# The MLP's first product by one level of Strassen's scheme, chunk after chunk

## The chip, the cores and the metric

The kernel runs on one core of a Trainium2 chip. Its time is the device time of one execution in microseconds: 1842.22 us, the median of three runs (1840.79 to 1843.36). TensorE (PE) multiplies matrices; VectorE (DVE), ScalarE (ACT) and GpSimd (POOL) do elementwise work; the queue of SyncE (SP) issues the transfers between DRAM and the on-chip memory SBUF. Each of the five has one stream of instructions and takes it in order. Sums of matrix products arise in PSUM, of which a bank holds 512 float32 values on each of 128 partitions.

## The reference

One layer of an encoder over 1536 tokens (512 of a prompt, 1024 of a sample) and 1024 channels, in float32:

```python
h = h + concat(o_attn, o_pool) @ w_out
m = rmsnorm(h, norm_mlp_g)
h = h + square(relu(m @ w_up)) @ w_down          # w_up 1024x4096, w_down 4096x1024
gate = sigmoid(rmsnorm(h, norm_ple_g) @ w_ple_gate)
h = h + gate * (p_i @ w_ple_proj)
```

Ahead of it stand a norm, an input projection, attention and a pooling mixer; behind it a final norm.

## The kernel before

Every matrix product is made as three passes of float32r matmuls: both operands are split into a high part (a cast) and a low part (the value less the cast), and high*high, high*low and low*high are summed (`three`). From the output projection on, activations lie transposed, channels on partitions: `hT[c][a]` is the residual stream of chunk c (512 tokens; chunk 0 the prompt, 1 and 2 the sample), channels 256a to 256a+255, as a tile of 128x1024. SBUF is one pool of 49 equal slots; a load into a slot waits for the slot's last reader, and loads stand in SP's queue in the order written.

`heads_out` adds the attention's rows of the output projection (`po`, matmuls of 128x256, each sum added to `h` by DVE). `mean_square(c)` squares a chunk's residual (`squares`: ACT squares, POOL sums, L581 to L591), splits the sum into `sh` (ACT L615, POOL L616), sums over partitions on TensorE (`w<-sh,ones_sb`) and takes it out by DVE (L621). The inverse root of it is not applied to the MLP's input: since the MLP is the square of a relu, the residual is multiplied by the mean square instead (`raise_h`, L630) and later by its inverse (`invert`, L637; `lower_h`, L644). `prep(c)` makes the two parts of the MLP's input (ACT L605, POOL or DVE L598); the norm's gain is multiplied into the weights (L740).

The MLP takes 32 hidden blocks f of 128 channels, and for each the three chunks in turn. `up(f, c)` is 8 x 3 matmuls of 128x512 into `pu`; ACT takes the relu (L757) and the square (L758, the high part of r), POOL squares again (L759), DVE makes the low part (L761). `down(f, c)` runs one step later: 4 x 2 x 3 matmuls of 128x512 into `pd`, and four DVE adds into the residual (L937). So a block's weights (one load of 512 KB each for up and down; split by ACT L743 and POOL L744) serve three chunks, and each is loaded once. The order of all this is written by hand in one list of pairs (f, c), with chores (generators that issue one step at a time) between.

Behind the MLP, `gate` makes the gated embedding: products `pj` and `pg` from `hg` (L1018, L1019), `wg` (L985, L986), `pp` and `wpj`; `stat_g` is the norm in front of it.

## Time and profile before

| what | value |
|---|---|
| median of runs | 1842.22 us (1840.79 to 1843.36) |
| profiled execution: span of its instructions | 1839.5 us |
| TensorE busy | 1806.2 us, 98% |
| DVE, ACT, POOL busy | 1098.3, 684.8, 652.8 us |
| MLP on TensorE, first `pu` to first `pj` | 575.05 to 1649.28 us |
| moved by DMA | 112.28 MB |

The profile page and the answers of the trace are of one execution, whose span is 1839.5 us; the runs' times are of the whole program and stand some 2.7 us above it. In a row of groups stand line, engine, operation, output and inputs, partitions x elements and the count; then busy time in us and mean ns of one (pipelined matmuls overlap, so their mean is longer than their spacing), then the idle time of the engine ahead of them and what ended it. In a timeline row stand the start and the length in us of a run of equal instructions, and in brackets the idle time ahead. "PEclk" or the clock column is the granted clock of TensorE as a share of the full one.

### The profile page before, as it was taken

The page shows a single profiled execution, that of the slowest core. Times are in us where ns is not written, and L with a number is a line of the kernel's source. Part 1 is how long each engine was busy: PE and PEld are TensorE (multiplying, and loading weights), DVE is VectorE, ACT ScalarE, POOL GpSimd, SP SyncE. Part 2 cuts the span into 40 slices and gives each one's busy share as a digit, 9 for nine tenths or more (in the row PEclk, how much of TensorE's full clock was granted, in tenths as well). Part 3 has the DMA queues.
Part 4 walks back from the last instruction along what each step waited for, and adds up shares of the span by engine and source line. Part 5 has one row for each costly group of instructions (what it writes and reads, how often), then busy time and mean ns, then how long its engine had stood idle before and what let it go on. Part 6 is the DMA issues. An engine that isn't in the chain of part 4 may idle for free.

```text
span 1839.5 us, 22941 instructions
## 1 busy us (share of the span) xinstructions
PE 1806.2 (98%) x8812; PEld 1492.1 (81%) x8812; DVE 1098.3 (60%) x1440; ACT 684.8 (37%) x1380; POOL 652.8 (35%) x611
## 2 busy tenths in 40 slices
...
DMA packets 34701, 112.28 MB, mean 61 GB/s; under 512 B 4768, under 2 KB 7200, under 8 KB 34592
## 3 DMA queue, kind: packets, MB, share of 16 engines
...
q14 instruction: 40, 0.33, 0.1%
...
## 4 chain that ended last, share of the span: by engine, by line
PE 88%; DVE 5%; issue 2%; ACT 2%; POOL 1%; DMA 0%; POOLq 0%; DVEq 0%; ACTq 0%
PE pd L49 28%; PE pu L49 27%; PE pg L49 7%; PE z L49 7%; PE o L49 3%; PE tp L53 3%; PE pp L49 3%; PE S L49 3%; PE po L49 3%; PE pj L49 2%; DVE m L598 1%; DVE wg L986 1%; DVE pt L473 1%; DVE nm L441 1%; PE py L49 0%
## 5 line engine op out<-in xcount | busy, mean ns | idle before, releaser
L937 DVE TENSOR_TENSOR h<-pd,h 128x1024 f32<-128x1024 f32 x372 | 445.9, 1219 | 497.0 <-PE pd L49 496.1
L49 PE MATMUL pd<-r,wd 128*128 128x512 f32 x2304 | 550.9, 394 | 3.2 <-DVE r L761 3.2
L49 PE MATMUL pu<-m,wu 128*128 128x512 f32 x2304 | 548.4, 393 | 0.0
L49 PEld LDWEIGHTS pd<-r,wd 128*128 128x128 f32 x2304 | 433.4, 188 | 104.9 <-DVE r L761 4.1
L49 PEld LDWEIGHTS pu<-m,wu 128*128 128x128 f32 x2304 | 432.8, 188 | 100.4
L759 POOL TENSOR_TENSOR ra<-ra 128x512 f32<-128x512 f32 x96 | 101.0, 1052 | 712.7 <-ACT r L758 702.8
L757 ACT ACTIVATE ra<-pu 128x512 f32<-128x512 f32 x96 | 57.4, 598 | 774.5 <-PE pu L49 774.5
L49 PE MATMUL z<-w,x 128*128 128x512 f32 (+1 forms) x864 | 175.9, 360 | 1.4 <-ACT w L159 1.4
L49 PEld LDWEIGHTS z<-w,x 128*128 128x128 f32 x864 | 143.7, 190 | 27.5 <-ACT w L159 2.8
L461 POOL TENSOR_SCALAR pr<-pr,rr 128x512 f32<-128x512 f32 x160 | 111.2, 705 | 128.0 <-DVE rr L456 62.8
L49 PE MATMUL pg<-hg,wg 128*128 128x512 f32 (+1 forms) x768 | 141.2, 338 | 1.8 <-POOL hg L1019 0.9
L49 PEld LDWEIGHTS pg<-hg,wg 128*128 128x128 f32 x768 | 118.4, 188 | 19.6 <-DVE wg L986 1.6
L473 DVE TENSOR_TENSOR pt<-tp,pt 128x512 fp32r<-128x512 f32 x160 | 104.0, 683 | 31.9 <-ACT pt L472 31.5
L472 ACT CAST pt<-tp 128x512 fp32r<-128x512 f32 x160 | 88.0, 591 | 86.2 <-PE tp L53 84.6
L441 DVE TENSOR_REDUCE nm<-S 128x1 f32<-128x1024 f32 (+1 forms) x96 | 100.0, 1042 | 23.6 <-PE S L49 23.0
L449 ACT ACTIVATE pr<-S,nm 128x512 f32<-128x512 f32 x160 | 109.5, 695 | 5.1 <-DVE nm L441 4.3
L744 POOL TENSOR_TENSOR wu<-wur,wu 128x1024 fp32r<-128x1024 f32 x32 | 78.2, 2443 | 80.4 <-ACT wu L743 75.9
L49 PE MATMUL o<-pt,vs 128*128 128x512 f32 x320 | 95.4, 407 | 2.6 <-DVE pt L473 2.2
L49 PE MATMUL S<-ks,qb 128*128 128x512 f32 x320 | 91.2, 398 | 1.8 <-DVE h L696 0.8
L53 PE MATMUL tp<-id_sb,pr 128*128 128x128 f32 x640 | 86.4, 273 | 3.7 <-DVE qs L343 3.3
L53 PEld LDWEIGHTS tp<-id_sb,pr 128*128 128x128 f32 x640 | 75.1, 140 | 18.1 <-issue 4.3
L761 DVE TENSOR_TENSOR r<-ra,r 128x512 fp32r<-128x512 f32 x96 | 68.7, 716 | 23.4 <-POOL ra L759 23.4
...
## 6 DMA issues: line engine op xcount, KB each, us to landing
wur<-in_w_up_dram SPq DMA_DIRECT2D x32, 512.0 KB, 3.3
wdr<-in_w_down_dram SPq DMA_DIRECT2D x32, 512.0 KB, 3.3
xn<-in_xn_dram SPq DMA_DIRECT2D x12, 512.0 KB, 6.5
qs_d<-qs SPq DMA_DIRECT2D x12, 512.0 KB, 3.0
yT_d<-y SPq DMA_DIRECT2D x12, 512.0 KB, 2.9
qb<-qs_d SPq DMA_DIRECT2D x12, 512.0 KB, 3.9
yb<-yT_d SPq DMA_DIRECT2D x12, 512.0 KB, 5.4
h<-in_xr_dram SPq DMA_DIRECT2D x12, 512.0 KB, 6.1
```

What stands on the lines that cost most here:

```text
L49: last_pe[0] = nc.tensor.matmul(*a, **k).ins
L53: last_pe[0] = nc.tensor.transpose(*a, **k).ins
L441: ve.tensor_reduce(nm, S[:, :nch * CH], axis=AX.X, op=ALU.max, negate=True)
L449: sc.activation(self.pr[j // 2, c][:, j % 2], S[:, c * CH:(c + 1) * CH], AF.Exp, bias=nm, accum_out=self.sums[:, j, c:c + 1])
L461: gp.tensor_scalar(p, p, rr, 1.0, op0=ALU.mult, op1=ALU.mult)
L472: sc.copy(self.pt[kt][:, 0], tp)
L473: ve.tensor_tensor(self.pt[kt][:, 1], tp, as32(self.pt[kt][:, 0]), op=ALU.subtract)
L744: gp.tensor_tensor(WM[f, i][1], raw, as32(WM[f, i][0]), op=ALU.subtract)
L757: sc.activation(a, pu, AF.Relu)
L759: gp.tensor_tensor(a, a, a, op=ALU.mult)
L761: low.append(lambda: ve.tensor_tensor(r[:, 1], a, as32(r[:, 0]), op=ALU.subtract))
L937: ve.tensor_tensor(hT[c][a], pd.rearrange("p (a b) -> p a b", a=2), hT[c][a], op=ALU.add)
```

## The change

The product of a pair of hidden blocks with a chunk's input is taken as a 2x2 block product: the contraction in halves of 512 channels, the hidden channels in halves of 128 (the two blocks), the tokens in halves of 256. Strassen's scheme in Winograd's form makes it of seven products of the quarters where eight are usual, with sums of the operands ahead and of the results behind. Numbers 1 to 7 name the products: each is 12 matmuls of 128x256.

- `operands(c)` makes the seven right operands of a chunk: ACT scales the normed gain into the residual copy `m` (eight steps of 128x512, L611), DVE forms the differences `t` (ten, L617), ACT casts (14, L622), POOL and DVE make the lows (seven each, L626). The gain has left the weights.
- `Pair.feed` makes the seven left operands of a pair: s1 to s4 on DVE (L785 to L796), seven casts on ACT (L778), seven lows on POOL (L779). `split_down` splits two blocks of the second product's weights (ACT L808; POOL and DVE L809).
- `Pair.run` writes the products to `px`, `py`, `pz`, `pq` (two products each add into `px`, `pz`, `pq`), ACT and DVE combine them in SBUF (`t`, u2, u4, c1, c2) and take relu, square and the low parts of r (L845 to L878).
- `Pair.down` sums the two blocks' rows of the second product in PSUM: again 48 matmuls of 128x512 per pair and chunk, with four adds (L829) where there were eight.
- Chunks run in turn: 16 pairs of chunk 0, then of 1, then of 2. All weights are loaded and split three times, 192 loads of 512 KB where there were 64. The residual of a finished chunk goes to DRAM (`hl_d`), those of the others come from there (`h_d`); the mean square goes there as soon as it is made (`w_d`, L654).
- In the last pair of chunk 0 and 1 the operands of the next chunk are made, between that pair's own steps.
- The first gate follows the last pair's `down` at once; the splits of `wpj`, `wg`, `pp` and `hg` stand between its four parts and behind them.

Three places of the order. POOL at the start of the MLP, before, from the split of block 1's weights on (`sqm` and `sh` belong to chunk 2's mean square, whose sum `w` stood on TensorE inside the third `up`; the first `up` followed the last `po` there):

```order
L744 TENSOR_TENSOR wu_1_6443<-wur_6262,wu_1_6442 128x1024
L744 TENSOR_TENSOR wd_1_6447<-wdr_6264,wd_1_6446 128x1024
L759 TENSOR_TENSOR ra_6490<-ra_6490 128x512
L589 TENSOR_TENSOR sqm_6485<-sqm_6485,sqm_6500 128x1024
L589 TENSOR_TENSOR sqm_6485<-sqm_6485,sqm_6508 128x1024
L589 TENSOR_TENSOR sqm_6485<-sqm_6485,sqm_6517 128x1024
L591 TENSOR_TENSOR sqm_6485<-sqm_6485 128x512
L759 TENSOR_TENSOR ra_6531<-ra_6531 128x512
L616 TENSOR_TENSOR sh_6573<-sqm_6485,sh_6573 128x512
```

and now, behind six lows of operands(0) (`mo_i1` is the low part of the operand of product i, `w_0_i` an operand from the weights of pair 0):

```order
L779 TENSOR_TENSOR w_0_1_6426<-wur_00_6057,w_0_1_6426 128x512
L626 TENSOR_TENSOR mo_41_6431<-t_6421,mo_40_6430 128x512
L779 TENSOR_TENSOR w_0_6_6437<-ws_00_6424,w_0_6_6437 128x512
L779 TENSOR_TENSOR w_0_2_6444<-wur_00_6057,w_0_2_6444 128x512
L589 TENSOR_TENSOR sqm_6440<-sqm_6440,sqm_6442 128x1024
L589 TENSOR_TENSOR sqm_6440<-sqm_6440,sqm_6447 128x1024
L779 TENSOR_TENSOR w_0_5_6453<-ws_00_6424,w_0_5_6453 128x512
L589 TENSOR_TENSOR sqm_6440<-sqm_6440,sqm_6450 128x1024
L591 TENSOR_TENSOR sqm_6440<-sqm_6440 128x512
L648 TENSOR_TENSOR sh_6463<-sqm_6440,sh_6463 128x512
L779 TENSOR_TENSOR w_0_7_6520<-ws_01_6425,w_0_7_6520 128x512
```

On TensorE the two matmuls `w` of chunk 2 now stand between the last `po` and the first `px`, so that POOL's `sh` is ahead of every product.

SP at the same place, before (`w_d` is stored from chunk 0's `sqm`):

```order
L56 DMA wur_6262<-in_w_up_dram 128x1024
L56 DMA wdr_6264<-in_w_down_dram 128x1024
L56 DMA wur_6741<-in_w_up_dram 128x1024
L56 DMA wdr_6743<-in_w_down_dram 128x1024
L639 DMA w_d_259<-sqm_4561 128x512
L639 DMA w_d_260<-sqm_5856 128x512
L56 DMA wur_6895<-in_w_up_dram 128x1024
L56 DMA wdr_6897<-in_w_down_dram 128x1024
L639 DMA w_d_261<-sqm_6485 128x512
```

and now (`h_d_3_273` is the last of chunk 2's residual; `h_6488` to `h_6494` are chunk 0's residual, `w_6496` its mean square, `wdr_ij` the second product's weights of pair i):

```order
L702 DMA h_d_3_273<-h_5459 128x1024
L56 DMA wur_10_6457<-in_w_up_dram 128x1024
L56 DMA wur_11_6458<-in_w_up_dram 128x1024
L56 DMA h_6488<-h_d_0_262 128x1024
L654 DMA w_d_261<-sqm_6440 128x512
L56 DMA h_6490<-h_d_1_263 128x1024
L56 DMA h_6492<-h_d_2_264 128x1024
L56 DMA h_6494<-h_d_3_265 128x1024
L56 DMA w_6496<-w_d_259 128x512
L56 DMA wdr_00_6498<-in_w_down_dram 128x1024
L56 DMA wdr_01_6499<-in_w_down_dram 128x1024
L56 DMA wdr_10_6570<-in_w_down_dram 128x1024
```

The store of chunk 2's mean square, which DVE's L653 releases, now stands ahead of the loads that the first pair needs.

DVE in the last pair of chunk 0, whose rows before had no like (a middle stretch of the same engine then: an add out of PSUM, two of each `down` ahead of the low of r):

```order
L621 TENSOR_SCALAR sqm_6485<-w_6594 128x512
L937 TENSOR_TENSOR h_6100<-pd_6606,h_6100 128x1024
L937 TENSOR_TENSOR h_6102<-pd_6614,h_6102 128x1024
L761 TENSOR_TENSOR r_6602<-ra_6601,r_6602 128x512
L937 TENSOR_TENSOR h_6104<-pd_6623,h_6104 128x1024
L937 TENSOR_TENSOR h_6106<-pd_6631,h_6106 128x1024
```

and now, from s4 of that pair to u4 (`t_9683`, `t_9686` and `mo_` belong to chunk 1's operands, `pd_140`, `pd_141` to the `down` of the pair before):

```order
L796 TENSOR_TENSOR ws_151_9510<-wur_150_9370,ws_150_9509 128x512
L626 TENSOR_TENSOR mo_11_9645<-m_1_9391,mo_10_9644 128x512
L829 TENSOR_TENSOR h_6488<-pd_140_9650,h_6488 128x1024
L850 TENSOR_TENSOR u_15_9608<-py_15_9664,u_15_9608 128x256
L617 TENSOR_TENSOR t_9683<-m_0_9390 128x512
L617 TENSOR_TENSOR t_9683<-m_1_9391 128x512
L617 TENSOR_TENSOR t_9686<-m_2_9392,t_9683 128x512
L617 TENSOR_TENSOR t_9686<-m_3_9393,t_9683 128x512
L626 TENSOR_TENSOR mo_61_9690<-t_9686,mo_60_9689 128x512
L809 TENSOR_TENSOR wd_1511_9633<-wdr_151_9492,wd_1510_9632 128x512
L626 TENSOR_TENSOR mo_21_9714<-m_3_9393,mo_20_9713 128x512
L829 TENSOR_TENSOR h_6490<-pd_141_9719,h_6490 128x1024
```

The rows of operands stand between the adds, u2 and u4; each `mo_` row waits for a cast of ACT, which in its queue stands behind the eight scales.

The diff, cut to its core:

```diff
+    def operands(c):
+        m = mraw.pop(c)
+        A, B = slice(0, HF), slice(HF, CH)
...
+        def quarter(half, tok):
+            return [m[2 * half + b][:, :, tok] for b in range(2)]
+        def scale(a, h):
+            sc.activation(m[a][:, h], m[a][:, h], AF.Copy, scale=gmlp_sb[:, 2 * a + h:2 * a + h + 1])
+        def minus(nm, x, y, b):
...
+            ve.tensor_tensor(T[nm][b], x()[b], y()[b], op=ALU.subtract)
+        def high(i, x, b):
...
+            sc.copy(MO[c][i][0][:, 2 * b:2 * b + 2], x()[b])
+        def low_(i, x, b):
+            hi, lo = (t[:, 2 * b:2 * b + 2] for t in MO[c][i])
+            (gp, ve)[b].tensor_tensor(lo, x()[b], as32(hi), op=ALU.subtract)
+        steps[0] = [lambda a=a, h=h: scale(a, h) for a in (0, 1, 2, 3) for h in range(2)]
+        b11, b12, b21, b22 = (lambda: quarter(0, A)), (lambda: quarter(0, B)), (lambda: quarter(1, A)), (lambda: quarter(1, B))
+        t = [lambda i=i: T[i] for i in range(5)]
+        sums = {6: ((1, b12, b11), (2, b22, t[1])), 7: ((3, b22, b12),), 4: ((4, b21, t[2]),)}
+        for i, x in ((1, b11), (6, t[2]), (2, b21), (5, t[1]), (7, t[3]), (3, b22), (4, t[4])):
+            for nm, p, q in sums.get(i, ()):
+                steps[i] += [lambda nm=nm, p=p, q=q, b=b: minus(nm, p, q, b) for b in range(2)]
+            for b in range(2):
+                steps[i] += [lambda i=i, x=x, b=b: high(i, x, b)]
+            for b in range(2):
+                steps[i] += [lambda i=i, x=x, b=b: low_(i, x, b)]
+        return steps
...
-        ws[c] = acc[:, 0]
+        sy.dma_start(w_d[c], acc[:, 0])
...
+                    chores.extend((mean_square(c, gp), spill(c)))
...
+        def feed(self):
+            def split(i, x):
+                t = self.w[i] = slot([P, 2, CH], F32R, f"w{self.id}_{i}")
+                sc.copy(t[:, 0], x)
+                gp.tensor_tensor(t[:, 1], x, as32(t[:, 0]), op=ALU.subtract)
+            (a11, a12), (a21, a22) = ((r[:, 0:CH], r[:, CH:D]) for r in self.raw)
+            s = [slot([P, 2, CH], F32, f"ws{self.id}{i}") for i in range(2)]
+            s1, s2, s3, s4 = s[0][:, 0], s[0][:, 1], s[1][:, 0], s[1][:, 1]
+            split(1, a11)
+            ve.tensor_tensor(s1, a21, a22, op=ALU.add)
+            yield
+            ve.tensor_tensor(s2, s1, a11, op=ALU.subtract)
+            split(6, s2)
+            yield
+            split(2, a12)
+            yield
+            split(5, s1)
+            ve.tensor_tensor(s3, a11, a21, op=ALU.subtract)
+            yield
+            split(7, s3)
+            ve.tensor_tensor(s4, a12, s2, op=ALU.subtract)
+            yield
+            split(3, s4)
+            yield
+            split(4, a22)
+            yield
+        def split_down(self):
+            self.wd = [[slot([P, D], F32R, f"wd{self.id}{i}{j}") for j in range(2)] for i in range(2)]
+            for i in range(2):
+                for h in (slice(0, CH), slice(CH, D)):
+                    hi, lo = (x[:, h] for x in self.wd[i])
+                    sc.copy(hi, self.dr[i][:, h])
+                    (gp, ve)[i].tensor_tensor(lo, self.dr[i][:, h], as32(hi), op=ALU.subtract)
+                    yield
...
+        def product(self, i, out, fresh=True):
+            w, m = self.w.pop(i), MO[self.c][i]
+            for k in range(4):
+                ws_ = [w[:, j, k * P:(k + 1) * P] for j in range(2)]
+                for j, (w_, m_) in enumerate(three(ws_, [x[:, k, :] for x in m])):
+                    pe.matmul(out, w_, m_, start=fresh and k == 0 and j == 0, stop=k == 3 and j == 2,
...
+        def down(self, a):
+            pd = ps("d", f"pd{self.id}{a}")
+            for e in range(2):
+                d = 2 * a + e
+                for f in range(2):
+                    ws_ = [w[:, d * P:(d + 1) * P] for w in self.wd[f]]
+                    for i, (w_, x_) in enumerate(three(ws_, [self.r[f][:, 0], self.r[f][:, 1]])):
+                        pe.matmul(pd[:, e * CH:(e + 1) * CH], w_, x_, start=f == 0 and i == 0, stop=f == 1 and i == 2)
+            h = hT[self.c][a]
+            ve.tensor_tensor(h, pd.rearrange("p (a b) -> p a b", a=2), h, op=ALU.add)
+        def run(self, between, after):
+            A, B = slice(0, HF), slice(HF, CH)
+            u = slot([P, 4, HF], F32, f"u{self.id}")
+            t, u2, u4 = u[:, 0], u[:, 1], u[:, 2]
+            c = slot([P, 2, CH], F32, f"c{self.id}")
+            c1, c2 = c[:, 0], c[:, 1]
+            self.r = [slot([P, 2, CH], F32R, f"r{self.id}{i}") for i in range(2)]
+            def bank(tag, nm):
+                return (tp_ps(f"{nm}{self.id}") if tag == "tp" else ps(tag, f"{nm}{self.id}"))[:, 0:HF]
+            x = bank("tp", "px")
+            self.product(1, x)
+            sc.copy(t, x)
+            after(1)
+            between(0)
+            y = bank("u", "py")
+            self.product(6, y)
+            ve.tensor_tensor(u2, y, t, op=ALU.add)
+            after(6)
+            self.product(2, x, False)
+            sc.activation(c1[:, A], x, AF.Relu)
+            after(2)
+            between(1)
+            z = bank("tp", "pz")
+            self.product(5, z)
+            ve.tensor_tensor(u4, z, u2, op=ALU.add)
+            after(5)
+            q = bank("u", "pq")
+            self.product(7, q)
+            ve.tensor_tensor(c2[:, B], q, u4, op=ALU.add)
+            after(7)
+            between(2)
+            self.product(3, z, False)
+            ve.tensor_tensor(c1[:, B], z, u2, op=ALU.add)
+            sc.activation(c1[:, B], c1[:, B], AF.Relu)
+            sc.activation(self.r[0][:, 0], c1, AF.Square)
+            sc.activation(c1, c1, AF.Square)
+            after(3)
+            self.product(4, q, False)
+            ve.tensor_tensor(c2[:, A], q, u2, op=ALU.add)
+            sc.activation(c2, c2, AF.Relu)
+            sc.activation(self.r[1][:, 0], c2, AF.Square)
+            sc.activation(c2, c2, AF.Square)
+            after(4)
+            for i, x in enumerate((c1, c2)):
+                ve.tensor_tensor(self.r[i][:, 1], x, as32(self.r[i][:, 0]), op=ALU.subtract)
+            between(3)
...
+    made = operands(0)
+    made = [act for i in (0, 1, 6, 2, 5, 7, 3, 4) for act in made[i]]
+    chores.append(steps_of(*[lambda i=i: [act() for act in made[i:i + 2]] for i in range(0, len(made), 2)]))
     while fill:
         fill.popleft()()
-        if len(fill) < 8:
-            step()
+        step(2)
+    for _ in range(4):
+        next(feeding)
+        step(2)
+    while chores:
+        step()
     ps_free()
     acc_free()
-    ps, ps_free = psum_tags(d=(2, 3))
-    split_mlp(1)
+    ps, ps_free = psum_tags(d=(2, 2), u=(1, 2))
...
+    for n, pair in enumerate(pairs):
+        c, g = pair.c, pair.g
+        made = {}
+        if g == 0:
+            for a in range(4):
+                load_h(c, a, h_d[c][a])
+            load_ms(c)
+            chores.append(raise_h(c))
+        if g == 1 and c:
+            load_ms(c - 1)
+        if g == NG - 1 and c < 2:
+            made = operands(c + 1)
...
+        def between(i):
+            if before:
+                before.down(i)
+            if i == 1 and n + 1 < len(pairs):
+                pairs[n + 1].load_down()
+        def after(i):
+            next(feeding, None)
+            next(splits, None)
+            if i == 1:
+                for act in made.get(0, ()):
+                    act()
+            for act in made.get(i, ()):
+                act()
             step()
-        up(f, c, f < 3)
-        if f > 1 and c == 0:
-            load_mlp(f + 1)
-        elif f > 1 and c == 1:
-            split_mlp(f + 1)
-        if i:
-            while order[i - 1][1] not in raised:
+        pair.run(between, after)
+        for _ in splits:
+            pass
+        if g == 0:
+            while chores:
                 step()
-            down(*order[i - 1])
...
-    load_p(0), load_p(1), load_g(0)
-    chores.extend((lower_w(0), steps_of(lambda: split_p(0), lambda: split_p(1), lambda: split_g(0))))
-    down2(LF - 1, 0, 3)
-    up(LF, 1, True)
-    low.popleft()()
-    for k in range(1, 4):
+        if g == 1 and c:
+            chores.extend((invert(c - 1), lower_h(c - 1, ve), stat_g(c - 1, ve), store_h(c - 1)))
+        before = pair
...
+    chores.append(steps_of(lambda: split_p(0), lambda: split_p(1), lambda: split_g(0)))
+    for k in range(1, KD):
         load_g(k)
     load_pp(0)
-    chores.extend((lower_h(0, ve), steps_of(*[lambda k=k: split_g(k) for k in range(1, 4)]), gate_in(0, gp, 1), stat_g(0, ve)))
-    up(LF - 1, 2, True)
-    down2(LF - 1, 1)
-    up(LF, 2, True)
-    for k in range(4, 8):
-        load_g(k)
-    late = gate_in(0, gp, 3)
-    chores.append(steps_of(lambda: next(late), lambda: next(late), lambda: split_g(4), lambda: split_g(5),
-                           lambda: next(late), lambda: split_g(6), lambda: split_g(7)))
-    down2(LF - 1, 2, 3)
+    late = gate_in(0, gp)
+    chores.append(steps_of(*[lambda: next(late) for _ in range(5)], *[lambda k=k: split_g(k) for k in range(1, KD)]))
+    for a in range(4):
+        before.down(a)
+        step(4)
```

191 lines of the change are left out of this document (68 added, 123 removed).

## The prediction

> **What bounds the kernel now.** I read the page first: engine shares, chain of waits, costliest groups.
>
> ```profile
> span 1839.5 us, 22941 instructions
> PE 1806.2 (98%) x8812; PEld 1492.1 (81%) x8812; DVE 1098.3 (60%) x1440; ACT 684.8 (37%) x1380; POOL 652.8 (35%) x611
> PE 88%; DVE 5%; issue 2%; ACT 2%; POOL 1%; DMA 0%; POOLq 0%; DVEq 0%; ACTq 0%
> L937 DVE TENSOR_TENSOR h<-pd,h 128x1024 f32<-128x1024 f32 x372 | 445.9, 1219 | 497.0 <-PE pd L49 496.1
> L49 PE MATMUL pd<-r,wd 128*128 128x512 f32 x2304 | 550.9, 394 | 3.2 <-DVE r L761 3.2
> L49 PE MATMUL pu<-m,wu 128*128 128x512 f32 x2304 | 548.4, 393 | 0.0
> ```
>
> TensorE is busy 98% of the span and carries the chain; the MLP's two products wait 3.2 us in all. Every vector engine has room on average. So the change can gain only matmul time, and it loses whatever it makes TensorE wait. The timeline of TensorE bounds the stretch, and the table by stretch gives its rate in the middle (columns: stretch; length and PE busy; PEld, DVE, ACT, POOL busy; clock; DMA share; GB/s).
>
> ```profile
> 565.21 10.00 PE L49 MATMUL po<-cat,wo 128*128 128x256 f32 x84
> 575.05 11.28 PE L49 MATMUL pu<-m,wu 128*128 128x512 f32 x48
> 588.75 3.51 PE L49 MATMUL pd<-r,wd 128*128 128x512 f32 x14 [2.19 <-DVE r L761]
> ...
> 1601.48 7.00 PE L49 MATMUL pd<-r,wd 128*128 128x512 f32 x29 [1.05 <-DVE r L761]
> ...
> 1649.28 1.54 PE L49 MATMUL pj<-pp,wpj 128*128 128x512 f32 x6
> ...
> 1656.08 0.50 PE L49 MATMUL pg<-hg,wg 128*128 128x512 f32 x1 [0.85 <-POOL hg L1019]
> 1657.16 0.96 PE L49 MATMUL pg<-hg,wg 128*128 128x512 f32 x3 [0.58 <-DVE wg L986]
> 1658.36 0.51 PE L49 MATMUL pg<-hg,wg 128*128 128x512 f32 x1 [0.24 <-DVE wg L986]
> ```
> ```profile
> 800.00:1000.00 200.00, 200.00 (x864) 162.16 (x863) 95.60 (x90) 48.21 (x96) 47.36 (x30) 1.00 0.10 32
> ```
>
> The MLP runs from 575.05 to 1649.28, 1074.2 us. A 512-wide matmul takes 200/864 = 0.2315 us; 4608 of them are 1066.8. The five bracketed waits, those of the first gate included, add up to 4.9 us. That is what the change has to beat.
>
> **The term it removes.** Per pair of hidden blocks and chunk, 48 matmuls of 512 (11.11 us) become 84 of 256. The row at 565.21 is just such a run: 84 in 10.00 us, 0.119 each, against 0.116 for half a 512. So 1.11 us per pair, times 48 pairs: **-53.4 us**. `down` keeps its 48 matmuls of 512 per pair, so a pair is 10.00 + 11.11 = 21.1 us of TensorE. The added loads (192 of 512 KB for 64) use queue time that the middle has free: the DMA share there is 0.10 and becomes about 0.3.
>
> ```profile
> wur<-in_w_up_dram SPq DMA_DIRECT2D x32, 512.0 KB, 3.3
> wdr<-in_w_down_dram SPq DMA_DIRECT2D x32, 512.0 KB, 3.3
> ```
>
> Four loads in a pair at 3.3 us are 13.2 of 21.1 even if none overlapped; I count them at nothing. Without that cover a pair would last as long as its loads.
>
> **A middle pair on the other engines.** Durations:
>
> ```profile
> L616 POOL TENSOR_TENSOR sh<-sqm,sh 128x512 fp32r<-128x512 f32 x1 | 1.3, 1293 | 0.0
> L615 ACT CAST sh<-sqm 128x512 fp32r<-128x512 f32 x1 | 0.6, 622 | 0.7 <-POOL sqm L591 0.7
> L588 ACT ACTIVATE sqm<-h 128x1024 f32<-128x1024 f32 x3 | 3.2, 1055 | 6.8 <-POOL sqm L589 6.8
> L985 ACT ACTIVATE wg<-wgr,gple_sb 128x1024 fp32r<-128x1024 f32 x6 | 6.6, 1143 | 0.0
> L717 DVE TENSOR_TENSOR h<-po,h 128x256 f32<-128x256 f32 x8 | 3.2, 416 | 2.7 <-PE po L49 2.7
> 588.02 0.68 DVE L761 TENSOR_TENSOR r<-ra,r 128x512 fp32r<-128x512 f32 x1
> 592.12 2.40 POOL L589 TENSOR_TENSOR sqm<-sqm,sqm 128x1024 f32<-128x1024 f32 x1 [1.17 <-ACT sqm L588]
> 561.90 0.41 ACT L506 CAST cat<-ob 128x256 fp32r<-128x256 f32 x1 [1.99 <-DVE ob L498]
> ```
>
> POOL: nine lows at 1.29 = 11.6. DVE: eight operations of 512 from SBUF at 0.68 (four sums, two wd lows, two r lows) = 5.4, five combinations at 0.42 and four adds at 1.22 = 7.0; 12.4. ACT: eleven casts and four squares at 0.6, two relus and a copy, 10.5. All fit into 21.1. The tight one is r: its last low is ready some 22.3 us after the pair's first product starts, and the first `down` that reads it stands at 23.5. About 1 us of slack, so no steady wait; I count 2 us for all pairs (0 to 10).
>
> **What goes wrong at the edges.** *Start.* In the old order products follow the last po directly, and chunk 2's mean square runs under them. Now `w` (its sum over partitions) stands ahead of the first product, behind operands(0), the first splits and the squares. ACT is free at 562.3 (its last cat cast), makes eight scales at about 0.64 (half of L985's with its start) until 567.4; then casts, DVE's differences and lows follow each other between po adds until about 580. From there POOL has four lows (5.2), two sums (4.8), a low (1.3), a sum (2.4), L591 (1.3), then ACT a cast (0.6) and POOL the low of sh (1.3), `w` 0.5, and two waits for ACT's squares, 1.055 each: 599.6, if nothing collides. TensorE's po is done at 575.0: 24.6 us of waiting. Collisions add to it. The same engines in the same place before:
>
> ```profile
> 573.41 1.21 DVE L598 TENSOR_TENSOR m<-h,m 128x1024 fp32r<-128x1024 f32 x1
> 576.68 11.41 DVE L598 TENSOR_TENSOR m<-h,m 128x1024 fp32r<-128x1024 f32 x4
> ...
> 565.82 2.42 POOL L744 TENSOR_TENSOR wu<-wur,wu 128x1024 fp32r<-128x1024 f32 x1 [2.70 <-ACT wu L743]
> 578.32 3.38 POOL L744 TENSOR_TENSOR wd<-wdr,wd 128x1024 fp32r<-128x1024 f32 x1
> 583.65 3.36 POOL L589 TENSOR_TENSOR sqm<-sqm,sqm 128x1024 f32<-128x1024 f32 x1
> ```
>
> Four DVE lows need 4.8 us alone and took 11.4 beside POOL, whose 2.4 became 3.4. The Trainium skill, page "SBUF — State Buffer", section "SBUF: two separate sides", has a rule that speaks against this change: a GpSimd operation and a VectorE operation with two SBUF inputs take turns on one pair of ports, each for its whole length. The rows agree; by it alone the edges cost the upper numbers below, by no such rule the lower.
>
> In the start DVE has about 20 such operations and POOL 16; I take **28** (24.6 to 32).
>
> *First pair.* SP stores w_d only after L653 (0.7 us behind `w`); three residual loads, chunk 0's w and the first wdr stand behind that store. A store and a load at 3.3 each put w and wdr 7 to 8 us behind `w`. DVE's queue holds four raises (1.2 each) between u2, u4 and c2B, and u4 frees what P3 writes next. There is no `down` to cover it: products of 10 us, lows and the first D0 end 12 later than they would; **12** (8 to 14).
>
> *Two changes of chunk.* In the last pair ACT has, behind the px copy, w_7, wd, eight scales and two casts: 7.3 us before DVE's row for mo_1 can go; D0's add, u2, u4 wait behind that row. Up to the r lows DVE then holds 25 operations of 512 at 0.62 spacing (15.5), three adds (3.7) and five combinations (2.1): 28.6, and waits for ACT's later casts that I add up to 7: 35.6, where the next pair needs r at 22.5. So 13.1 each without collisions; POOL's 18 lows (23 us) over the same 35 make it up to 22. I take 19 each, nearer to the crowded rows above: **38**, and **3** for the late pair behind each (0 to 6).
>
> *Tail.* The last `down`s are followed by the gate at once; before, two more up/down rounds covered its preparation. POOL has wpj, pp, hg: seven of 128x1024, 16.8 us at 2.40; DVE eight wg lows, 9.8 at the 1.22 of the adds, one behind the other if they collide as the lows above did. From 22 us after the last pair's start, with a cast of ACT ahead, that ends at about 49.8; the pair (21.1), its own `down` (11.1) and the gate's first 30 matmuls (7.0) would end at 39.3: **10.5** (0.7, if the two run side by side, to 12). The two sums for the gate's norms between: **2** (0 to 4).
>
> *Clock.* After a window in which TensorE idles the granted clock is about half (columns: stretch; length and PE busy; clock; DMA share; GB/s), and at half a stretch holds 10 matmuls of 512 for 20:
>
> ```profile
> 7.42:10.83 3.41, 3.41 (x10) 0.50 0.96 383
> 10.83:14.24 3.41, 3.41 (x20) 1.00 0.94 338
> ...
> 1826.00:1829.40 3.40, 0.33 (x5) 1.00 0.46 154
> 1829.40:1832.80 3.40, 1.78 (x8) 0.61 0.46 154
> ```
>
> That is 1.7 us lost each time. Start, first pair, chunk changes and tail make three to four: **6** (2 to 12).
>
> **The sum.** Added waits 28 + 12 + 38 + 3 + 10.5 + 2 + 6 + 2 = 101.5; less the 4.9 of before, less 53.4: +43.2. On the profiled 1839.5 that is 1882.7; the median stands 2.7 above the profiled span, so 1885. All lower ends (24.6, 8, 26.2, 0, 0.7, 0, 2, 0 = 61.5) give +3.2, 1845; all upper ends (32, 14, 44, 6, 12, 4, 12, 10 = 134) give +76, 1918.
>
> **Rivals.**
>
> *The edges are hidden.* If the mean square and the operands of the next chunk run under products that are already there, the saving stands: 1842 - 53.4 and some 15 of waits left = 1804. For it: DVE, ACT and POOL are 60, 37 and 35% busy on the page, and a pair has 8 us free on each. Against it: each engine keeps its written order, and in that order `w` stands ahead of the first product, and mo_1 ahead of D0's add. It decides if the edges cost under 50 in all; even without one collision I reach 61.5. Chance 0.10, for errors in chains as long as these.
>
> *Ports bind every pair.* DVE 5.4 and POOL 11.6 us of operations that exclude each other are 17 of 21.1. If a low of r meets a POOL low (1.29) each time and loses the 1 us slack with 1 more, 45 pairs add 45 us: 1930. Before, the r lows were hardly disturbed,
>
> ```profile
> L761 DVE TENSOR_TENSOR r<-ra,r 128x512 fp32r<-128x512 f32 x96 | 68.7, 716 | 23.4 <-POOL ra L759 23.4
> ```
>
> 0.716 on average to the 0.68 of one alone, but POOL was busy 47.36 of 200 us there, 5.0 in the time of a pair. Chance 0.15. The rule named above from the Trainium skill ("SBUF — State Buffer") would give this case, if turns fall badly.
>
> *256-wide matmuls at a slower rate.* The grouped row below, its time shared over the count, has 0.135 each; the saving is gone at 0.132.
>
> ```profile
> L49 PE MATMUL po<-cat,wo 128*128 128x256 f32 x576 | 77.7, 287 | 0.0
> ```
>
> At 0.135 a pair gains nothing and loses 0.2: 1885 + 53 + 11 = 1949. The group is broken up by transposes, the run of 84 is not, and products are runs of 12 between others of their kind; chance 0.05. If only the saving fails this decides at once, whatever the edges.
>
> *The loads stall.* Three times the loads with slots freed late: a stalled pair loses up to 3.3 us; 5 in all would be 1900. Chance 0.05, inside the range.
>
> **How the numbers follow.** My sum 0.65, edges hidden 0.10, ports 0.15, slow matmuls 0.05, loads 0.05. A measurement here tells 0.2% (3.7 us) from no change. Faster takes the hidden edges, 0.10, and a sliver of my sum, 0.01; the same 0.04, from the low corner of the sum; slower 0.85. The likeliest case's own range is 1845 to 1918; the range 1840 to 1930 leaves the hidden edges below (0.09), and half of the port case and the slow matmuls above (0.12): two in ten.
>
> **What would show it.** Runs of 12 products at 1.43 us and a pair of 21.1 with TensorE full: the saving. A gap of 25 to 32 us ahead of the first px that ends on `w`; clock 0.50 behind it; gaps at P3 and at the first `down` in the two changes of chunk that end on DVE's u or r; gate waits on hg or wg. It is wrong if the edges add up to under 50 us, if middle pairs show waits for r, or if a product run takes 1.6 us.

## The result, and the profile after

The changed kernel takes 1887.6 us (1887.37 to 1887.94), beside 1842.8 us (1840.79 to 1843.62) for the kernel before: a ratio of 1.0248, with a 95% interval of 1.0233 to 1.0262. It is slower, and 1885 was forecast. The profiled spans are 1885.6 and 1839.5 us, 46.1 apart; the medians are 44.8 apart, since the profiled execution of the kernel before was a short one (the median stands 3.3 above that span, the changed kernel's 2.0 above its own).

First the page of the changed kernel: span, engines, and the chain of waits.

```profile
span 1885.6 us, 28256 instructions
PE 1772.4 (94%) x10540; PEld 1552.4 (82%) x10540; DVE 1246.7 (66%) x1829; ACT 937.7 (50%) x1830; POOL 1013.9 (54%) x888
...
PE 56%; DVE 5%; ACT 2%; issue 2%; POOL 1%; DMA 0%; POOLq 0%; DVEq 0%; SPq 0%; ACTq 0%
```

TensorE is busy 33.8 us less than before, and still the end comes 46.1 us later. The averages of DVE, ACT and POOL look harmless (66, 50 and 54%). Where TensorE stands still is told by its waits (columns: what waits for what; us in total, times, longest):

```profile
PE w L49 <- ACT sh L647: 26.3, 1, 26.3
PE pz L49 <- DVE u L858: 21.0, 3, 8.1
PE pd L49 <- DVE r L878: 19.3, 5, 8.8
PE pg L49 <- DVE h L829: 11.1, 1, 11.1
```

Ten waits make 77.7 us. They stand at the edges, as TensorE's timeline shows for the long ones (start, length, work, and in brackets the idle time ahead):

```profile
605.88 0.79 PE L49 MATMUL w<-sh,ones_sb 128*128 128x512 f32 x1 [26.27 <-ACT sh L647]
...
607.82 2.76 PE L49 MATMUL px<-mo,w 128*128 128x256 f32 x12
...
625.20 2.90 PE L49 MATMUL pz<-mo,w 128*128 128x256 f32 x12 [8.05 <-DVE u L858]
...
951.37 2.90 PE L49 MATMUL pz<-mo,w 128*128 128x256 f32 x12 [6.48 <-DVE u L858]
969.78 5.08 PE L49 MATMUL pd<-r,wd 128*128 128x512 f32 x11 [8.02 <-DVE r L878]
...
1329.75 5.46 PE L49 MATMUL pd<-r,wd 128*128 128x512 f32 x11 [8.79 <-DVE r L878]
...
1609.97 2.93 PE L49 MATMUL pd<-r,wd 128*128 128x512 f32 x12
1631.05 2.94 PE L49 MATMUL pd<-r,wd 128*128 128x512 f32 x12
...
1683.03 1.57 PE L49 MATMUL pj<-pp,wpj 128*128 128x512 f32 x6
1695.72 8.35 PE L49 MATMUL pg<-hg,wg 128*128 128x512 f32 x24 [11.12 <-DVE h L829]
```

The waits stand at the start of the MLP, in its first pair, around the two changes of chunk (951 and 970; 1330 is the second of the other) and ahead of the gate; two of 0.74 and 0.77 us stand in the third pair of chunks 1 and 2, where the finished chunk's norm is made. The rows at 1609.97 and 1631.05 are the same point of two neighbouring middle pairs, 21.08 us apart. The table by stretch has no idle time in the middle, and shows the granted clock (columns: stretch; length and PE busy; PEld, DVE, ACT, POOL busy; clock; DMA share; GB/s):

```profile
1100.00:1300.00 200.00, 200.00 (x1257) 180.13 (x1256) 116.47 (x158) 100.46 (x188) 119.15 (x86) 1.00 0.34 110
...
581.80:612.50 30.70, 6.07 (x24) 5.47 (x25) 10.86 (x14) 10.95 (x17) 20.33 (x13) 0.50 0.33 114
...
619.30:633.00 13.70, 6.19 (x27) 5.96 (x28) 9.96 (x12) 5.61 (x12) 9.53 (x6) 0.50 0.43 159
947.00:957.20 10.20, 5.76 (x25) 5.53 (x26) 9.52 (x12) 4.24 (x8) 6.73 (x6) 0.50 0.05 15
963.80:974.00 10.20, 4.18 (x9) 2.91 (x10) 9.18 (x9) 5.42 (x11) 7.04 (x6) 0.51 0.27 109
1308.80:1315.60 6.80, 4.26 (x18) 4.03 (x19) 6.80 (x10) 1.39 (x4) 3.33 (x4) 0.50 0.00 0
1325.90:1336.10 10.20, 6.32 (x17) 4.73 (x18) 8.10 (x8) 3.71 (x8) 8.57 (x6) 0.50 0.21 67
1687.70:1701.30 13.60, 5.58 (x13) 4.45 (x14) 11.46 (x7) 0.00 (x0) 5.66 (x2) 0.50 0.08 17
```

In the order of the prediction's sum, with what the two traces have:

| term | forecast | measured |
|---|---|---|
| 48 pairs of products | -53.4 | about -54 (22.22 to 21.1 a pair) |
| last `po` to first `px` | 28 (24.6 to 32) | 28.2 (579.6 to 607.8) |
| first pair, waits | 12 (8 to 14) | 10.6 (8.05, 1.61, 0.95) |
| two changes of chunk, waits | 38 (26.2 to 44) | 29.8 (6.48, 8.02; 6.50, 8.79) |
| pairs with the finished chunk's norm | 3 + 2 | 4.6 (22.3, 22.4; 22.3, 22.0 for 21.1), the waits of 0.74 and 0.77 in it |
| ahead of the gate | 10.5 (0.7 to 12) | 11.1 |
| half clock | 6 (2 to 12) | about 19 |
| middle pairs, waits | 2 (0 to 10) | 0 |
| up to the last `po`, and behind the gate | not in the sum | 4.5 + 0.9 |
| waits and other work that stood there before | -4.9 | -9.3 |
| sum | +43.2 | +46.1 |

The -9.3 is what the old MLP lasted beyond its matmuls, 1074.2 - 48 x 22.22 = 7.6, and the gate's waits of before, 1.7. For half clock 19.7 us then remain. The trace gives nearly the same without the sum: in the seven rows at about half clock TensorE is busy 38.4 us, work that takes about half of that at the full clock, so some 19 us are lost (an estimate): 10 at the two changes, 3 at the start, 3 in the first pair, 3 in the gate.

### The profile page after: what moved, and what is told of

Same layout as the page of the kernel before. It is cut to its first block, busy times and chain, and to the rows that moved or that the text cites. A ratio compares the mean times of both kernels' runs of the same rounds, so it can differ in the third digit from the quotient of the medians.

```text
span 1885.6 us, 28256 instructions
## 1 busy us (share of the span) xinstructions
PE 1772.4 (94%) x10540; PEld 1552.4 (82%) x10540; DVE 1246.7 (66%) x1829; ACT 937.7 (50%) x1830; POOL 1013.9 (54%) x888
## 4 chain that ended last, share of the span: by engine, by line
PE 56%; DVE 5%; ACT 2%; issue 2%; POOL 1%; DMA 0%; POOLq 0%; DVEq 0%; SPq 0%; ACTq 0%
PE pd L49 26%; PE pz L49 7%; PE pq L49 7%; PE px L49 6%; PE pg L49 5%; PE py L49 3%; PE pj L49 1%; DVE h L1241 1%; DVE r L878 1%; DVE wg L1085 1%; DVE h L829 1%; DVE wd L809 0%; DVE mo L626 0%; DMA w<-w_d 0%; DVE h L675 0%
## 5 line engine op out<-in xcount | busy, mean ns | idle before, releaser
L779 POOL TENSOR_TENSOR w<-ws,w 128x512 fp32r<-128x512 f32 x192 | 273.7, 1430 | 235.3 <-ACT w L778 226.4
L829 DVE TENSOR_TENSOR h<-pd,h 128x1024 f32<-128x1024 f32 x192 | 234.4, 1221 | 112.1 <-PE pd L49 112.1
L779 POOL TENSOR_TENSOR w<-wur,w 128x512 fp32r<-128x512 f32 x144 | 212.3, 1487 | 177.0 <-ACT w L778 175.3
L778 ACT CAST w<-ws 128x512 fp32r<-128x512 f32 x192 | 118.6, 618 | 245.4 <-DVE ws L787 214.3
L49 PEld LDWEIGHTS pz<-mo,w 128*128 128x128 f32 x1152 | 153.3, 193 | 30.2 <-issue 22.0
L49 PE MATMUL pz<-mo,w 128*128 128x256 f32 x1152 | 156.5, 286 | 21.0 <-DVE u L858 21.0
L49 PEld LDWEIGHTS z<-w,x 128*128 128x128 f32 x864 | 142.4, 188 | 28.2 <-ACT w L159 2.1
L809 DVE TENSOR_TENSOR wd<-wdr,wd 128x512 fp32r<-128x512 f32 x96 | 99.5, 1036 | 98.1 <-ACT wd L808 91.7
L49 PE MATMUL pq<-mo,w 128*128 128x256 f32 x1152 | 155.4, 285 | 1.8 <-DVE c L862 1.6
L49 PE MATMUL px<-mo,w 128*128 128x256 f32 x1152 | 153.5, 283 | 0.0
L49 PE MATMUL pg<-hg,wg 128*128 128x512 f32 (+1 forms) x768 | 142.6, 341 | 11.1 <-DVE h L829 11.1
L49 PEld LDWEIGHTS px<-mo,w 128*128 128x128 f32 x1152 | 148.1, 191 | 4.2
L49 PEld LDWEIGHTS pq<-mo,w 128*128 128x128 f32 x1152 | 146.2, 193 | 2.6 <-issue 2.5
L49 PEld LDWEIGHTS pg<-hg,wg 128*128 128x128 f32 x768 | 120.7, 191 | 28.9 <-issue 11.5
L809 POOL TENSOR_TENSOR wd<-wdr,wd 128x512 fp32r<-128x512 f32 x96 | 127.2, 1325 | 6.0 <-ACT wd L808 6.0
L878 DVE TENSOR_TENSOR r<-c,r 128x512 fp32r<-128x512 f32 x96 | 77.7, 815 | 70.1 <-ACT c L875 56.1
```

Of the source, the lines that this page charges most:

```text
L49: last_pe[0] = nc.tensor.matmul(*a, **k).ins
L778: sc.copy(t[:, 0], x)
L779: gp.tensor_tensor(t[:, 1], x, as32(t[:, 0]), op=ALU.subtract)
L809: (gp, ve)[i].tensor_tensor(lo, self.dr[i][:, h], as32(hi), op=ALU.subtract)
L829: ve.tensor_tensor(h, pd.rearrange("p (a b) -> p a b", a=2), h, op=ALU.add)
L878: ve.tensor_tensor(self.r[i][:, 1], x, as32(self.r[i][:, 0]), op=ALU.subtract)
```

## The experiments

Theory of the prediction: the matmuls saved are real, and the loss lies in four edges where a written order puts work of the new scheme ahead of what TensorE needs next. Rivals: the edges are slow since DVE's and POOL's operations take turns (then moving work helps little), and POOL's extra work holds every pair up. All ratios are to the kernel before, on the same chip. "Less" compares the median with the changed kernel's 1887.6, across several chips, on which the kernel before lies at 1842.3 to 1843.8; and in eight of these kernels, whose instructions are the same up to the last `po`, that group's last matmul starts at 577.5 to 581.2 us of the profile. So a difference of 2 us between two of them says little.

**One edge at a time.** e1: the mean square of chunk 2 and the store of its residual are issued from the second pair on (`held` is an empty list made at the start; n counts the pairs):

```diff
-                    chores.extend((mean_square(c, gp), spill(c)))
+                    (held if c == 2 else chores).extend((mean_square(c, gp), spill(c)))
...
+        if n == 1:
+            chores.extend(held)
```

> The mean square of chunk 2 and its spill are issued in the second and third pair and no longer ahead of the first product; nothing else is changed. Theory (the written order costs the start): the first px waits only for the lows of mo_1 and w_1, which in the changed kernel end at 587.2, so it starts some 20 us earlier; the raises of the first pair no longer wait for a store behind L653, and less time is spent at half clock: 24 to 34 us less, about 1858. Rival (the vector engines have too much work there, whatever its order): the same work stalls pairs 1 and 2 instead, at most 10 us less, 1877 or more.

Measured: 1872.14 us, 1.0151 (1.0134 to 1.0167), 15.5 below the changed kernel, between the two numbers expected. TensorE's timeline in this kernel:

```profile
584.93 0.80 PE L49 MATMUL px<-mo,w 128*128 128x256 f32 x2 [5.11 <-ACT w L779]
...
605.93 2.90 PE L49 MATMUL pz<-mo,w 128*128 128x256 f32 x12 [4.20 <-DVE u L859]
...
640.54 0.80 PE L49 MATMUL pd<-r,wd 128*128 128x512 f32 x1 [2.25 <-ACT r L875]
```

The first product starts 22.9 us earlier, although it now waits 5.11 for its own operand. Of the 22.9 only 15.5 are left at the end: px and py wait another 4.8 for the operands from the weights, and in the second pair comes a wait of 2.25 for a square on ACT that stands behind ACT's part of `sh`. The wait for u is shorter than it was, 4.20 for 8.05. So the mean square was the cause of the long wait, and it covered others.

e2: at a change of chunk, the next chunk's input is loaded one pair earlier and its eight scales are made in the pair before the last:

```diff
-        if g == NG - 1 and c < 2:
-            made = operands(c + 1)
         if g == NG - 2 and c < 2:
+            nxt = operands(c + 1)
+            for k, i in enumerate((1, 6, 2, 5, 7, 3, 4)):
+                made[i] = nxt[0][k:k + 1] if k < 6 else nxt[0][k:]
+        if g == NG - 1 and c < 2:
+            made = nxt
+            made[0] = []
+        if g == NG - 3 and c < 2:
             load_m(c + 1)
```

> The residual of the next chunk is loaded one pair earlier and ACT's eight scales are issued in the pair before the last. Theory (in the last pair mo_1 stands behind eight scales, and D0's add, u2 and u4 behind mo_1): the wait ahead of P3 (6.5 us at each change of chunk) goes, the one at the first down that reads r (8.0 and 8.8) stays or shrinks by the rest of the 5 us: 8 to 12 us less in all, about 1878. Rival (what counts is the amount of work that VectorE and GpSimd have in that pair): the wait moves to the r lows, at most 3 us less, 1885.

Measured: 1881.99 us, 1.0210 (1.0194 to 1.0225), 5.6 less. Little more than half of what the theory asked for, and the rows say which part came:

```profile
950.30 2.90 PE L49 MATMUL pz<-mo,w 128*128 128x256 f32 x12 [4.20 <-DVE u L858]
968.81 4.82 PE L49 MATMUL pd<-r,wd 128*128 128x512 f32 x11 [8.37 <-DVE r L878]
```

The wait for u falls from 6.48 to 4.20, so ACT's scales made 2.3 of it. The wait for r does not fall; it is 8.4 where it was 8.0. What DVE has to do in that pair has not become less.

e3: POOL's half of the operands' lows in chunks 1 and 2 is filled with zeros, so that POOL reads nothing there:

```diff
-            (gp, ve)[b].tensor_tensor(lo, x()[b], as32(hi), op=ALU.subtract)
+            if c and not b:
+                gp.memset(as32(lo), 0.0)
+            else:
+                (gp, ve)[b].tensor_tensor(lo, x()[b], as32(hi), op=ALU.subtract)
```

> In the operands of chunks 1 and 2 the half of the low parts that GpSimd makes is filled with zeros by a memset, which reads nothing (their values are left out of the products). Theory (operations of the two engines take turns): seven of GpSimd's sixteen operations in each last pair no longer hold up VectorE, whose rows of 128x512 there get 0.3 us shorter on average; 2 to 4 us less at each change of chunk, 4 to 8 in all, about 1881. Rival (no turns, the length of the queues alone): VectorE's rows keep their length and the time is within 2 us of 1887.6.

Measured: 1876.52 us, 1.0179 (1.0164 to 1.0195), 11.1 less, more than either number. Groups of DVE at the first change (930 to 975 us), in the changed kernel and then in this one:

```profile
L626 DVE TENSOR_TENSOR mo<-m,mo 128x512 fp32r<-128x512 f32 x3 | 3.9, 1291 | 9.2 <-ACT mo L622 9.2
```
```profile
L629 DVE TENSOR_TENSOR mo<-m,mo 128x512 fp32r<-128x512 f32 x3 | 2.2, 728 | 9.2 <-ACT mo L622 9.2
L627 POOL MEMSET mo<- 128x512 f32 x7 | 3.7, 528 | 0.0
```

The same three DVE instructions take 728 ns instead of 1291 once POOL does not read operands beside them. That the two engines hold each other up is therefore a true part of the price of a change: up to 11.1 us for two. It is an upper number, since the memsets (0.53 us) are also shorter than the lows that they replace (1.5), and this run does not part the two. The waits that stay, 4.4 for u and 6.3 to 7.5 for r, are DVE's queue with its waits for ACT's casts.

e4: the last add ahead of the gate. The steps of the gate's preparation (splits of `wpj`, `wg`, `pp` and `hg`) between the last four `down`s are moved behind them:

```diff
     for a in range(4):
         before.down(a)
-        step(4)
```

> Behind the last pair the four parts of down are issued without the steps of the gate's preparation between them, which follow; on VectorE the last add then stands ahead of the lows of wg. Theory (the gate's first pg waits for a PSUM bank, that the last add frees, and this add stood behind four lows of wg): the wait of 11.1 us becomes several short ones for wg and hg, 4 to 6 us less, about 1882. Rival (the splits of wg and hg, which take turns, are late themselves): pg ends as late as before, at most 2 us less, 1886.

Measured: 1879.91 us, 1.0198 (1.0183 to 1.0213), 7.7 less, more than the 4 to 6 expected. In the changed kernel DVE and POOL stood like this at the end:

```profile
1681.60 12.84 DVE L1085 SCALAR_TENSOR_TENSOR wg<-wgr,gple_sb,wg 128x1024 fp32r<-128x1024 f32 x4
1694.37 1.21 DVE L829 TENSOR_TENSOR h<-pd,h 128x1024 f32<-128x1024 f32 x1
...
1681.10 12.26 POOL L1113 TENSOR_TENSOR hg<-h,hg 128x1024 fp32r<-128x1024 f32 x4
```

The gate's pg at 1695.72 follows the add that begins at 1694.37 and empties `pd`'s bank of PSUM. That add stood behind four lows of `wg`, which needed 12.84 us, 3.2 each, beside POOL's four `hg`. With the adds first, TensorE waits for the lows themselves, in small pieces:

```profile
1683.90 0.95 PE L49 MATMUL pg<-hg,wg 128*128 128x512 f32 x3 [0.73 <-DVE wg L1085]
...
1687.21 0.98 PE L49 MATMUL pg<-hg,wg 128*128 128x512 f32 x3 [2.36 <-DVE wg L1085]
...
1690.52 6.48 PE L49 MATMUL pg<-hg,wg 128*128 128x512 f32 x16 [2.33 <-DVE wg L1085]
```

These are 5.4 us where there were 11.1. From the start of the last `down`s to the end of the first part's pg the two profiles differ by 4.9 us (30.1 for 35.0), so some 2.8 of the 7.7 lie elsewhere. All eight lows take DVE 14.21 us there, 1.8 each:

```profile
1682.23 14.21 DVE L1085 SCALAR_TENSOR_TENSOR wg<-wgr,gple_sb,wg 128x1024 fp32r<-128x1024 f32 x8
```

**An edge put right as a whole.** If order is the cause, each edge must give back most of its price when its work is spread over pairs that have room. e5: at the start, the eight scales go under the last scores of the attention, the mean square and the store of the residual into pairs 2 to 5 (`slow` puts an empty step between two of a chore's), the splits of the first weights between the operands, the operands 3 and 4 into the first pair, and chunk 0's raises into the second (`first_ops` are chunk 0's operands, `feed_` makes the next operand of the weights):

```diff
+        if at >= 98:
+            for act in made[0][2 * (at - 98):2 * (at - 97)]:
+                act()
...
+                        held.extend((slow(mean_square(c, gp), 2), spill(c)))
...
+    made = [feed_, *made[0][8:], *made[1], feed_, *made[6], feed_, *made[2], feed_, *made[5], *made[7]]
...
+            made = {1: first_ops[3], 6: first_ops[4]}
...
+            if g == 1:
+                next(raising, None)
```

> The start of the MLP alone is put in another order: the mean square of chunk 2 is spread over pairs 2 to 5, the eight scales are issued under the last scores of the attention, the first pair's weights are split between the operands, the operands of products 3 and 4 are made inside the first pair, and chunk 0's raises stand in pair 1, each ahead of its add. No work is left out. Theory (written order): the first px starts at about 581 for 607.8 and the waits of 8.1 for u4 and 1.6 behind it go: 28 to 40 us less, about 1853. Rival (amount of work on the vector engines): not over 5 us better than moving the mean square alone, which gave 1872: 1867 or more.

Measured: 1861.42 us, 1.0102 (1.0087 to 1.0117), 26.2 less, just short of the 28 to 40 expected. The first product comes at 580.3; what stays is 3.24 for an add of `po` and 8.46 for u4, since DVE's row for operand 3 stood there waiting for a cast of ACT, which stood behind a cast of `wd`, whose load came late.

e6: the changes of chunk: the load two pairs ahead, scales and differences in the pair before the last, two operands and the raises in the next chunk's first two pairs (the digits are the products behind which a step stands):

```diff
         if g == NG - 2 and c < 2:
+            nxt = operands(c + 1)
+            made = {1: nxt[0][:4], 6: nxt[0][4:], 2: nxt[6][:2], 5: nxt[6][2:4], 7: nxt[7][:2] + nxt[4][:2]}
+        if g == NG - 1 and c < 2:
+            made = {1: nxt[1], 6: nxt[6][4:], 2: nxt[2], 5: nxt[5], 7: nxt[7][2:]}
+        if g == 0 and c:
+            made = {1: nxt[3], 6: nxt[4][2:]}
```

> The two changes of chunk alone: the next chunk is loaded two pairs ahead, its scales and differences are made in the pair before the last, the operands of 1, 6, 2, 5 and 7 in the last pair, those of 3 and 4 in the first pair of the next chunk, and the raises one pair later. The number of operations is the same. Theory (each change costs 20 us because 25 VectorE rows and the casts they wait for stand in one pair): both waits, for u and for r, fall under 2 us: 25 to 36 us less, about 1857. Rival (collisions and amount, which come along wherever the rows stand): the pairs beside get waits for r, at most 12 us less, 1875 or more.

Measured: 1869.06 us, 1.0138 (1.0121 to 1.0155), 18.5 less: above the rival's 12, under the theory's 25. The longest wait of the first change is now 2.99, for c; the others are under 1.2.

e7: the tail: the splits of `wpj` and of two parts of `wg` go into the last pair, the lows of `hg` to DVE, each behind the add of its part:

```diff
+            made = {1: [lambda: split_p(0)], 6: [lambda: split_p(1)]}
+            made |= {i: [lambda k=k: split_g(k)] for k, i in list(enumerate((5, 7)))}
...
+    late = gate_in(0, ve)
...
         before.down(a)
-        step(4)
+        next(late)
+        for _ in range((len(left) + 3 - a) // (4 - a)):
+            split_g(left.pop(0))
```

> The tail alone: wpj and the first two wg are split in the last pair, VectorE makes the lows of hg in place of GpSimd, and the splits stand behind the adds of the four parts of down. Theory (first the add behind the lows, then the late lows): of the three waits of 5.4 us that were left with the adds first nearly all goes: 10 to 13 us under the changed kernel, about 1876. Rival (the lows are late in any order): no better than 1880, as with the adds first alone.

Measured: 1879.92 us, 1.0201 (1.0186 to 1.0216), 7.7 less, no more than e4's single line gave: the rival's number. Waits of 0.81, 0.41 and 3.77 stay, the last again for an add, behind `hg` and `wg` in DVE's row.

e8: all three together, with nothing else changed (the raises of every chunk in its second pair):

> The three of this set together. Theory (the 100 us of waits lie at these places and are due to where work was written): the gains add, 63 to 89 us under the changed kernel, about 1813, which is 30 under the kernel before. Rival (total work or turns on the ports bind once the gaps are shut): steady pairs get longer than 21.1 us and the time stays above 1840.

Measured: 1839.73 us, 0.9988 (0.9979 to 0.9998). The three gave 26.2 + 18.5 + 7.7 = 52.4 apart and 47.9 together: the edges are nearly independent. That is 0.1% from the kernel before, and 27 us short of the theory's 1813: apart as together, the three gave less than expected. The rival's time (above 1840) is nearly met, but not its reason: it blamed steady pairs, and the middle ones stay 21.1 us with no wait. What remains are edges again (8.9 us for u in the first pair, fifteen waits of up to 1.2 for r).

**Further spreading.** e9 puts the operands first in a chunk's first pair and the splits of the second product's weights from its product 5 on (the fourth in order), makes half of the scales one pair earlier, splits a third part of `wg` in the last pair, and lets the residual's stores take their turn in the list of loads:

```diff
-            next(splits, None)
+            if g or i in (5, 7, 3, 4):
+                next(splits, None)
...
+        if g == NG - 3 and c < 2:
+            load_m(c + 1)
+            nxt = operands(c + 1)
+            made = {4: nxt[0][:4]}
...
-            sy.dma_start(h_d[c][a], hT[c][a])
+            load(h_d[c][a], hT[c][a])
```

> The three places again, with what the set before left: in a chunk's first pair the operands stand ahead of the splits of wd (whose loads come late), the operands of 7, 3 and 4 of chunk 0 and of 5, 7, 3 and 4 of the others are made there; scales and differences of the next chunk stand behind P4, P1, P6 and P2 only, where VectorE has idle time, over three pairs; three wg are split in the last pair; chunk 2's residual is stored in its turn instead of ahead of the loads. No work is left out. Theory (waits come from where rows stand; middle pairs keep 21.1 us): of the waits left (some 16 us at the start, 9 at each change of chunk, 5 at the tail, half clock with them) half or more goes: 1815 to 1827. Rival (turns on the ports take back what is spread): 1835 or more, the same as the three together before.

Measured: 1856.19 us, 1.0065 (1.0051 to 1.0078). A miss in the wrong direction, 16.5 above e8. TensorE at the first pair and after the first change, and DVE's row between:

```profile
608.14 5.09 PE L49 MATMUL pd<-r,wd 128*128 128x512 f32 x11 [7.49 <-DVE r L888]
...
964.83 5.46 PE L49 MATMUL pd<-r,wd 128*128 128x512 f32 x11 [6.08 <-DVE r L888]
```
```profile
961.77 1.34 DVE L819 TENSOR_TENSOR wd<-wdr,wd 128x512 fp32r<-128x512 f32 x1 [2.45 <-ACT wd L818]
963.03 3.42 DVE L888 TENSOR_TENSOR r<-c,r 128x512 fp32r<-128x512 f32 x2
```

The splits of wd, now late, stand ahead of the two lows of r. DVE sits idle 2.45 us for a cast that belongs to one of them, and both lows of r, for which `down` waits, come behind. Three such waits, of 7.49, 6.08 and 6.04, are back.

e10: so in a chunk's first pair the splits go back to every place between the products, but behind the operands of the same place; the tail is again that of e7; the scales move to the fourth and third pair from a chunk's end, and four operands are left for the next chunk's first pair:

```diff
-            next(splits, None)
+            if g:
+                next(splits, None)
...
             for act in made.get(i, ()):
                 act()
+            if not g:
+                next(splits, None)
...
+        if g == NG - 2 and c < 2:
+            made = {1: nxt[6][:2], 6: nxt[6][2:4], 2: nxt[7][:2]}
+        if g == NG - 1 and c < 2:
+            made = {1: nxt[1], 6: nxt[6][4:], 2: nxt[2]}
+        if g == 0 and c:
+            made = {1: nxt[5], 6: nxt[7][2:], 2: nxt[3], 5: nxt[4]}
```

> The three places together once more, in the order that the two runs before suggest: splits of wd stay where they were in each pair but behind the operands in a chunk's first pair; scales behind P4 of the third and fourth pair from the end, differences behind P1, P6 and P2 of the pair before the last, operands of 1, 6 and 2 in the last pair, of 5, 7, 3 and 4 in the next chunk's first; the tail as in its own run; chunk 2's residual stored in its turn. No work is left out. Theory (a row costs where it stands ahead of u4 or of a low of r, and nothing elsewhere): both changes of chunk under 6 us of waits, the start under 10: 1822 to 1834. Rival (the amount of VectorE and GpSimd work around these places sets it): 1838 or more, like the three together before.

Measured: 1832.65 us, 0.9947 (0.9934 to 0.9959), as expected: 0.5% below the kernel before.

e12: last, one of operand 4's differences goes into the last pair, and the finished chunk's norm is spread to one step in two places (the expectation says three; `slow` with 2 puts one empty step between):

```diff
-            made = {1: nxt[1], 6: nxt[6][4:], 2: nxt[2]}
+            made = {1: nxt[4][:2] + nxt[1], 6: nxt[6][4:], 2: nxt[2]}
...
-            chores.extend((invert(c - 1), lower_h(c - 1, ve), stat_g(c - 1, ve), store_h(c - 1)))
+            chores.extend((slow(invert(c - 1), 2), slow(lower_h(c - 1, ve), 2), slow(stat_g(c - 1, ve), 2), store_h(c - 1)))
```

> The run before with two moves more: the last difference (t4) of the next chunk stands behind P1 of the last pair instead of behind P5 in the first pair of the next chunk, and the finished chunk's steps (inverse, lowering, squares for the gate's norm) are issued one in three places, over some nine pairs instead of three. No work is left out. Theory (a row costs only where it stands ahead of a combination or an r low that TensorE needs next): the wait of 3.4 ahead of P4 at each change of chunk shrinks by half, the three pairs behind it, 22.0, 23.5 and 22.5 us in the run before, come near 21.3: 6 to 12 us less than 1832.65, 1821 to 1827. Rival (the same VectorE time is lost in smaller parts): 1830 to 1835.

Measured: 1827.68 us (1825.52 to 1829.32), 0.9917 (0.9904 to 0.9931), just past the end of the range expected and below both kernels. Its page and TensorE's waits:

```profile
span 1826.7 us, 28221 instructions
PE 1768.4 (97%) x10540; PEld 1545.8 (85%) x10540; DVE 1280.7 (70%) x1833; ACT 935.7 (51%) x1830; POOL 1018.3 (56%) x884
```
```profile
PE pq L49 <- DVE c L872: 9.8, 5, 5.0
PE pz L49 <- DVE u L868: 5.7, 5, 2.4
...
PE pg L49 <- DVE h L839: 3.8, 1, 3.8
PE pd L49 <- DVE r L888: 3.5, 7, 0.8
```

The busy times are those of the changed kernel, within 0.5% on TensorE, ACT and POOL; DVE is 34 us busier, and four lows of `hg` have gone from POOL to it. The four largest groups of waits in the MLP and the gate make 22.8 us where they made 77.7; the time at half clock there has fallen too, from 28 stretches of 3.4 us to 6. The time has fallen by 59.9 with no work left out: the order did that.

**Does POOL bind every pair?** e11: two of POOL's nine lows per pair are made twice in the changed kernel; the second time rewrites the same values:

```diff
+                for _ in range(2 if i in (2, 5) else 1):
+                    gp.tensor_tensor(t[:, 1], x, as32(t[:, 0]), op=ALU.subtract)
```

> The changed kernel with two of GpSimd's nine lows in each pair made twice (the second writes the same values): 2.6 us more of GpSimd work with two reads in all 48 pairs, 14.2 of 21.1 us. Theory (middle pairs have room on every engine, and r has about 1 us): the middle pairs stay at 21.1 us or lose some tenths; the start, where GpSimd's rows stand ahead of the squares, and the changes of chunk lose up to 2 each: 1888 to 1905. Rival (turns on the ports nearly bind a pair): 1 us or more in each of 45 pairs, over 1930.

Measured: 1904.27 us, 1.0338 (1.0322 to 1.0354), 16.7 above the changed kernel, just inside the theory's end and far from the rival's 1930. The middle stretch:

```profile
1100.00:1300.00 200.00, 200.00 (x1256) 180.09 (x1255) 134.25 (x164) 94.84 (x178) 142.77 (x104) 1.00 0.32 109
```

POOL rises from 119 to 143 of 200 us. DVE, which has nothing more to do, rises with it from 116.47 (158 rows) to 134.25 (164): 0.737 to 0.819 us an instruction. So DVE's instructions do lengthen with POOL's work in middle pairs, as turns would have it, and TensorE does not notice: 200.00 of 200. What is lost is lost at the edges and next to them: the wait for `sh` grows from 26.3 to 28.9, those for r at the changes from 8.0 and 8.8 to 10.8 and 10.5, and in the first five pairs behind each change small waits for r come to 4.2 and 3.7 us where they were 0.7 and 0.8.

## Why the prediction was right, point by point

**The saving** was as costed: 21.08 us between the same points of neighbouring middle pairs for the 21.1 forecast. The runs of 12 matmuls come at 0.119 each; the rival of slower 256-wide matmuls falls. The loads stayed hidden as forecast: a DMA share of 0.34 for about 0.3, and no wait of a middle pair for one; that rival falls too. The other engines' work in a pair was as listed (12.3, 10.6 and 12.6 us of DVE, ACT and POOL in 21.1, from the middle row, for 12.4, 10.5 and 11.6).

**The start** came out at 28.2 for 28, and the timeline shows the chain forecast, but the number is partly luck. POOL's lows of the operands and the first splits, its sums and then ACT's and POOL's parts of sh stand ahead of `w`:

```profile
585.48 1.71 POOL L779 TENSOR_TENSOR w<-wur,w 128x512 fp32r<-128x512 f32 x1
...
605.91 1.27 POOL L648 TENSOR_TENSOR sh<-sqm,sh 128x512 fp32r<-128x512 f32 x1 [0.73 <-ACT sh L647]
```

Experiment e1 moved the mean square away, and the wait for `w` was gone. But both ends of the gap lie later than worked out. The sixth operand low of POOL ends at 585.5 where "until about 580" stands, and the four lows behind it take 10.1 us for 5.2, since POOL idles 4.3 among them for ACT's casts; the steps from the sums on take 11.6 for 11.7, and the two waits for squares did not come. So the first px starts at 607.8, where 28 us behind 575.0 would be 603. TensorE's `po` ends 4.6 us later too, which keeps the gap at 28.2: about 3 us at the end of the attention, and 1.1 in two waits of `po` for adds behind the operands in DVE's row; the share of chance in it is some 2 us, by the eight profiles named above. "TensorE's po is done at 575.0" took the end of before for given, though the change puts new rows ahead of it.

**The first pair** waited 10.6 for 12, for the reason given. DVE's raise waits for the load of chunk 0's mean square, whose place in SP's queue is behind the store of chunk 2's, and u4 is behind the raise:

```profile
616.93 1.22 DVE L664 TENSOR_TENSOR h<-h,w 128x1024 f32<-128x1024 f32 x1 [7.58 <-DMA w<-w_d]
```

**The changes of chunk** cost 14.5 and 15.3 in waits, where 13.1 was worked out without collisions, 22 with, and 19 taken. The places were right, too (u4, then the low of r). In the profile of the changed kernel the parts of the chain can be read off DVE:

```profile
938.26 1.37 DVE L626 TENSOR_TENSOR mo<-m,mo 128x512 fp32r<-128x512 f32 x1 [5.80 <-ACT mo L622]
...
950.81 0.41 DVE L858 TENSOR_TENSOR u<-pz,u 128x256 f32<-128x256 f32 x1
...
967.98 3.43 DVE L878 TENSOR_TENSOR r<-c,r 128x512 fp32r<-128x512 f32 x2
```

From ACT's px copy at 930.87 to mo_1 at 938.26 pass 7.4 us, forecast as 7.3 (DVE is idle for 5.80 of them); then come lows of 1.37 and 1.7 us that take 0.7 alone. Experiments e2 and e3, each by itself, put ACT's scales at 5.6 us for two changes and POOL's share at up to 11.1; that DVE's length makes the rest is argued, not shown by a run of its own. The rule cited from the Trainium skill ("SBUF — State Buffer", "SBUF: two separate sides") agrees with e3's 728 against 1291 ns.

**Half clock** is the term that was mis-sized: 6 us, for three or four windows at 1.7, where about 19 were lost. The working took one window of half clock per edge. The trace has seven places, since each change has two long waits, and at each the clock is full again only 4.3 to 6.6 us after TensorE has begun to work (951.37 to 957.2, 1311.27 to 1315.6, 605.88 to 612.5); in the first pair, where a second wait of 1.61 follows, it takes 7.8. Half of the busy time in between is lost, 2.1 to 3.2 us at each place. The bound of 12 was too low for the same reason. The changes' lower waits (29.8 for 38) make up for more than half of this; the sum of the two is 49 for 44. That the total came so near is thus in part luck.

**The tail** had the right size, 11.1 for 10.5, and the wrong cause. The step "POOL has wpj, pp, hg ... DVE eight wg lows ... the gate's first 30 matmuls" has the gate waiting for its operands. It waited for a bank of PSUM, which an add behind four of these lows had yet to empty (e4). With the add out of the way the operands alone cost 5.4 us, about half of the forecast, so that the number came out alike is luck. What the working had right is that the lows of `wg` lengthen beside POOL's `hg` (3.2 us each); four of these set the add's delay.

**The rivals.** "The edges are hidden" falls for the order as written; e12 shows that another order does hide most of them, at 1827.7, where 1804 had been worked out for 15 us of waits. "Ports bind every pair" falls: with 20% more POOL work (e11) the middle pairs are as long as before. DVE's instructions do lengthen there, but r has the time that the prediction had called slack (about 1 us). In a middle pair of the changed kernel, on DVE and on TensorE:

```profile
1100.51 0.69 DVE L878 TENSOR_TENSOR r<-c,r 128x512 fp32r<-128x512 f32 x1 [1.73 <-ACT c L875]
```
```profile
1101.17 2.94 PE L49 MATMUL pd<-r,wd 128*128 128x512 f32 x12
```

The second low of r ends at 1101.20. The first three of these matmuls read the first block's part alone and the fourth the high part of the second, so the fifth, which is the first to need this low, comes at about 1102.1, some 0.9 us later. The 2 us for such waits in all pairs were 0.

What is open: the half clock's cost is read from the trace, and no run changes it alone; how much of the price of a change is turns and how much is the length of the queues was not parted; and the 19 us that e12 still waits for c, u and r, at the start and the changes, were not traced further.
